# Order of the 512-column and 256-column matmuls within each piece of up-projection weights

## The chip, the cores and the metric

The kernel runs on one core of one Trainium2 chip. The metric is device time in microseconds (us), as the median of the runs made. Lower is better.

## What is computed

One transformer block on 256 rows of width 2048: three kinds of attention with gates, an output projection, and a gated feed-forward part with a causal convolution. The change lies in the feed-forward part, of which the reference says

```python
h2 = rms_norm(x, g_ffn[l])
u = causal_depthwise_conv(h2 @ w_up[l], conv_w[l], conv_b[l])
u_gate, u_val = jnp.split(u, 2, axis=-1)
x = x + (jax.nn.silu(u_gate) * u_val) @ w_down[l]
```

`h2` is 256 x 2048, `w_up` 2048 x 11264, `w_down` 5632 x 2048, all in fp32.

## The kernel before

**Split operands.** Every operand of a big product is split into two parts of the reduced-precision type `float32r`: `hi` is the rounded value and `lo` the rest. A product is then hi x hi + hi x lo + lo x hi. Weights arrive in pieces of 128 x 1024 numbers (512 KB): `piece` issues the DMA into `raw` on SP's queue (L135), casts it to `hi` on ScalarE (L136) and subtracts to get `lo` on VectorE (L137). There are four buffers of each of `raw`, `hi` and `lo`.

**The up projection** (the stage called u, tiles `u`, `hi_u`, `lo_u`, `raw_u`; L729 to L745). It works transposed: the weights are the stationary operand, the hidden rows `hT` the moving one. For each of the 16 blocks of the depth 2048, `hT[:, k, :]` has 512 columns, the 256 hi ones and then the 256 lo ones. So one matmul with `hi` weights over 512 columns (L739) makes hi x hi in the first half of a PSUM bank and hi x lo in the second half; one matmul with `lo` weights over the 256 hi columns (L740) adds lo x hi to the first half. The two halves are added later.

The loops, from outside: 11 steps `f0` of four column blocks; `s` = 0 for the gate half and 1 for the value half (22 groups in all); eight pieces per group, each holding two depth blocks `j` of 512 weight columns; in a piece, four column blocks `i`, each with a PSUM bank of its own. A piece is thus 16 matmuls, eight of 512 columns and eight of 256, each with its own load of 128 x 128 weights: 176 pieces, 1408 + 1408 matmuls.

**After a group**, `conv` (L706 to L727) takes each of the four banks: ScalarE copies the second half (L710), VectorE adds the first (L712) and multiplies by the row norms (L713), three instructions apply the taps (L716 on ScalarE, L717 and L718 on VectorE), then silu (L720) or the product with the gate half (L724) and a split into `aT` (L169, L170). These steps are queued by `later` and handed out by `tick`, which runs once per piece.

**What sets the order.** TensorE, ScalarE and VectorE each run their own queue in order. The program is written in one order, and the framework's scheduler may move instructions of different tiles past each other on an engine, by times that it works out itself. So an edit of TensorE's order can shift what stands in ScalarE's and VectorE's queues. A cast into a `hi` or `lo` buffer waits until TensorE has read the buffer's earlier contents. There are eight PSUM banks; a group takes four, so a bank is needed again two groups later.

After the u stage comes the down projection (tiles `x`, `y`, `hi_d`, `lo_d`; L796 to L844), with 512-column matmuls throughout. Ahead of it lie the attention stages; the gate products (tiles `g`, L147 to L149) are 512-column matmuls in a row, and the last projection of the second attention (tile `s`, L147 to L149) has a part that is 256 columns wide, 96 such matmuls in a row.

Of the kernel before, what the change touches and what calls it, by code (L numbers as in the profile page):

```python
# [16 lines left out]
S = 256  # L17
NT = S // P
D = 2048
KT = D // P  # L20
# [21 lines left out]
def hybrid_block(  # L42
# [25 lines left out]
    nc = tc.nc  # L68
# [12 lines left out]
    def bank(name):  # L81
        return pp.tile([P, 512], F32, tag="bank", name=name)
# [14 lines left out]
    def later(gen):  # L97
        waiting.append(gen)

    def tick():  # L100
        while waiting and len(active) < WINDOW:
            active.append([waiting.popleft(), 0])
        for a in list(active):
            if a[1] > 0:
                a[1] -= 1
                continue
            try:
                a[1] = next(a[0]) or 0
            except StopIteration:
                active.remove(a)  # L110
# [19 lines left out]
    def piece(src, a, n, name):  # L130
        raw = wp.tile([P, PIECE], F32, tag="raw", name=f"raw_{name}")
        hi = wp.tile([P, PIECE], F32R, tag="hi", bufs=SBUFS, name=f"hi_{name}")
        lo = wp.tile([P, PIECE], F32R, tag="lo", bufs=SBUFS, name=f"lo_{name}")
        m = a * n
        nc.sync.dma_start(raw[:, :m].rearrange("p (a n) -> p a n", a=a), src)  # L135
        pin(nc.scalar.copy(hi[:, :m], raw[:, :m]))  # L136
        pin(nc.vector.tensor_tensor(lo[:, :m], raw[:, :m], hi[:, :m].bitcast(F32), ALU.subtract))  # L137
        return (
            hi[:, :m].rearrange("p (a n) -> p a n", a=a),
            lo[:, :m].rearrange("p (a n) -> p a n", a=a),  # L140
        )
# [9 lines left out]
    def product(x_of, w, nk, n0, n, name):  # L151

        ps = [bank(f"{name}_{t}") for t in range(NT)]
        wv = w.rearrange("(k p) n -> p k n", p=P)
        for k in range(0, nk, 2):
            a = min(2, nk - k)
            wh, wl = piece(wv[:, k : k + a, n0 : n0 + n], a, n, f"{name}_{k}")
            order = [(j, t) for j in range(a) for t in range(NT)]
            if k + a == nk:
                order.sort(key=lambda jt: jt[1])  # L160
            for j, t in order:
                passes(ps[t][:, :n], x_of(k + j), t, wh[:, j], wl[:, j], k + j == 0, k + j == nk - 1)
            tick()
        return ps
# [278 lines left out]
    ps = proj(C_MQ, MEM_W, "mq")  # L443
# [33 lines left out]
    for c in range(3):  # L477
        ps = proj(c * 512, 512, f"f{c}")
# [7 lines left out]
    ps = proj(1536, 512, "f3")  # L486
# [3 lines left out]
    ps = proj(2048, 262, "f4")  # L490
# [68 lines left out]
    for c in range(3):  # L559
        ps = proj(C_SB + c * 512, 512, f"s{c}")  # L560
# [4 lines left out]
    ps = proj(C_SB + 1536, 512, "s3")  # L565
# [3 lines left out]
    ps = proj(C_SB + 2048, 256, "s4")  # L569
# [61 lines left out]
    for n in range(4):  # L631
        n0 = n * 512
        gate = []
        for b in range(3):
            bg = gp.tile([P, 512], F32, tag="bg", name=f"bg_{n}_{b}")
            nc.sync.dma_start(bg, b_gate[0, b, n0 : n0 + 512].partition_broadcast(P))
            ps = proj(C_GATE + b * D + n0, 512, f"g{n}_{b}")
# [11 lines left out]
        for i, (w, k0, nk, b) in enumerate(branches):  # L649
            ps = product(lambda k: oT[:, k0 + k], w[0], nk, n0, 512, f"b{n}_{b}")  # L650
# [10 lines left out]
    hT = xt_pool.tile([P, KT, 2 * S], F32R, tag="xt", name="hT")  # L661
# [19 lines left out]
    for n in range(4):  # L681
        c = slice(n * 512, (n + 1) * 512)
        ps = product(lambda k: mT[k // 2][:, k % 2], w_out[0], KT, n * 512, 512, f"o{n}")
# [21 lines left out]
    def conv(ps, f, s):  # L705
        if not pads:  # L706
            padded()
        ct = s * FT + f
        cr = cp.tile([P, S], F32, tag="cr", bufs=2, name=f"cr_{f}_{s}")
        nc.scalar.copy(cr, ps[:, S:])  # L710
        u = pads[f % 2]
        nc.vector.tensor_tensor(cr, cr, ps[:, :S], ALU.add)  # L712
        nc.vector.tensor_tensor(u[:, 2:], cr, rbc, ALU.mult)  # L713
        y = cp.tile([P, S], F32, tag="y", bufs=6, name=f"y_{f}_{s}")
        tap = lambda j: taps[:, j, ct : ct + 1]
        nc.scalar.activation(y, u[:, 2:], AF.Identity, scale=tap(2), bias=tap(3))  # L716
        nc.vector.scalar_tensor_tensor(y, u[:, 1 : S + 1], tap(1), y, ALU.mult, ALU.add)  # L717
        nc.vector.scalar_tensor_tensor(y, u[:, 0:S], tap(0), y, ALU.mult, ALU.add)  # L718
        if s == 0:
            nc.scalar.activation(y, y, AF.Silu)  # L720
            ys[f] = y
        else:
            g = ys.pop(f)
            nc.vector.tensor_tensor(g, g, y, ALU.mult)  # L724
            split_to(aT[:, f, :], g)
        return
        yield  # L727

    for f0 in range(0, FT, 4):  # L729
        for s in range(2):  # L730
            ps = [bank(f"u{f0 + i}_{s}") for i in range(4)]
            c0 = s * D_FF + f0 * P
            for k in range(0, KT, 2):
                hi, lo = piece(upv[:, k : k + 2, c0 : c0 + 512], 2, 512, f"u{f0}_{s}_{k}")
                for j in range(2):
                    first, last = k + j == 0, k + j == KT - 1
                    for i in range(4):
                        c = slice(i * P, (i + 1) * P)
                        nc.tensor.matmul(ps[i], lhsT=hi[:, j, c], rhs=hT[:, k + j, :], start=first, stop=False)  # L739
                        nc.tensor.matmul(  # L740
                            ps[i][:, :S], lhsT=lo[:, j, c], rhs=hT[:, k + j, :S], start=False, stop=last
                        )
                tick()
            for i in range(4):
                later(conv(ps[i], f0 + i, s))  # L745
# [180 lines left out]
```

## Time and profile before

| | |
|---|---|
| median of 3 runs | 1499.82 us (1497.26 to 1500.45) |
| span of the profiled execution, first to last instruction | 1494.4 us |
| TensorE clock granted over the span | 1.000 |
| TensorE weight loads busy | 84% |
| VectorE busy, ScalarE busy | 68%, 53% |
| HBM read | 280.23 MB, 189 GB/s over the span |

The profile is of one execution. What the whole execution takes beyond the span is not on the page; against the median of the runs it is 1499.82 - 1494.4 = 5.4 us. In the profile a matmul's duration is a latency: the next one starts long before the last has ended, so the pace of a stream of matmuls is the distance from one start to the next, not the duration. PE stands for matmuls, PEld for weight loads, DVE for VectorE, ACT for ScalarE.

### The profile page before, as it was taken

Reading aid. Unit: us, or ns where it says so; the run is one execution under the profiler, and the core shown is the slowest. Engines: PE = TensorE matmul, PEld = TensorE weight load, DVE = VectorE, ACT = ScalarE, POOL = GpSimd, SP = SyncE. Lnnn points to the kernel's source line nnn. Section 1 sums busy time; section 2 is a strip of 40 time slices with the busy share of each in tenths; the row PEclk is TensorE's granted clock in tenths of the full one; section 3 lists DMA queues with packets and bytes.
Section 4 is the critical chain, followed back from the end, with each engine's and each line's share of the span. In section 5 each row is a group of like instructions: output and inputs, shape, how many; then the busy total and the mean of one; then the engine's idle time right before and its main releaser. Section 6 shows DMA issues by size and latency. Waiting matters only on the chain.

```text
span 1494.4 us, 19871 instructions
## 1 busy us (share of the span) xinstructions
PE 1483.2 (99%) x7429; PEld 1255.9 (84%) x7429; DVE 1014.0 (68%) x1465; ACT 794.0 (53%) x1108; POOL 16.1 (1%) x46
## 2 busy tenths in 40 slices
PE   8999999999999999999999999999999999999998
PEld 6888888888888888888888888888888888888777
DVE  5767566555655646555557778777778778987885
ACT  6755454358544444444456556556556656553552
POOL 0000000001000000000000000000000000000000
PEclk9999999999999999999999999999999999999999
DMA  8665475365666666655555665655656565556554
GB/s 291 193 211 158 126 220 167 119 211 164 188 194 210 185 210 203 185 190 190 184 182 183 198 191 184 196 190 184 198 187 191 186 196 183 199 188 228 185 202 140
DMA packets 138543, 283.62 MB, mean 190 GB/s; under 512 B 9275, under 2 KB 18127, under 8 KB 138447
## 3 DMA queue, kind: packets, MB, share of 16 engines
q1 hardware_dynamic: 137118, 280.26, 59.0%
q10 hardware_dynamic: 1328, 2.11, 0.4%
q8 instruction: 58, 0.95, 0.2%
q14 instruction: 39, 0.31, 0.1%
HBM read 280.23 MB, written 2.10 MB: 189 GB/s over the span
## 4 chain that ended last, share of the span: by engine, by line
PE 95%; DMA 2%; ACT 1%; DVE 1%; issue 0%; POOL 0%; SPq 0%; DVEq 0%; POOLq 0%; ACTq 0%
PE u L739 21%; PE u L740 11%; PE g L147 5%; PE g L148 5%; PE g L149 5%; PE x L797 4%; PE x L798 4%; PE x L799 4%; PE s L147 2%; PE s L149 2%; PE f L147 2%; PE f L149 2%; PE s L148 2%; PE f L148 2%; PE o L147 2%; PE o L149 2%
## 5 line engine op out<-in xcount | busy, mean ns | idle before, releaser
L739 PE MATMUL u<-hT,hi_u 128*128 128x512 f32 x1408 | 488.5, 392 | 0.0
L740 PE MATMUL u<-hT,lo_u 128*128 128x256 f32 x1408 | 395.1, 281 | 0.0
L739 PEld LDWEIGHTS u<-hT,hi_u 128*128 128x128 f32 x1408 | 263.3, 187 | 57.3
L137 DVE TENSOR_TENSOR lo_u<-raw_u,hi_u 128x1024 fp32r<-128x1024 f32 x176 | 215.4, 1224 | 116.0 <-ACT hi_u L136 115.9
L740 PEld LDWEIGHTS u<-hT,lo_u 128*128 128x128 f32 x1408 | 266.8, 189 | 0.0
L136 ACT CAST hi_u<-raw_u 128x1024 fp32r<-128x1024 f32 x176 | 184.7, 1050 | 138.4 <-PE u L739 106.5
L137 DVE TENSOR_TENSOR lo_g<-raw_g,hi_g 128x1024 fp32r<-128x1024 f32 x96 | 117.7, 1229 | 101.3 <-ACT hi_g L136 98.8
L136 ACT CAST hi_g<-raw_g 128x1024 fp32r<-128x1024 f32 x96 | 100.7, 1051 | 121.8 <-PE g L148 97.4
L147 PE MATMUL g<-hi_g,xT 128*128 128x512 f32 x384 | 151.1, 393 | 0.0
L149 PE MATMUL g<-lo_g,xT 128*128 128x512 f32 x384 | 149.8, 390 | 0.0
L148 PE MATMUL g<-hi_g,xT 128*128 128x512 f32 x384 | 149.7, 390 | 0.0
L792 ACT CAST hi_d<-raw_d 128x1024 fp32r<-128x1024 f32 (+1 forms) x88 | 86.7, 993 | 74.6 <-PE x L798 38.7
L793 DVE TENSOR_TENSOR lo_d<-raw_d,hi_d 128x1024 fp32r<-128x1024 f32 (+1 forms) x88 | 99.8, 1148 | 16.2 <-ACT hi_d L792 16.2
L797 PE MATMUL x<-hi_d,aT 128*128 128x512 f32 x268 | 104.4, 390 | 0.0
L799 PE MATMUL x<-lo_d,aT 128*128 128x512 f32 x268 | 104.4, 390 | 0.0
L798 PE MATMUL x<-hi_d,aT 128*128 128x512 f32 x268 | 104.4, 390 | 0.0
L149 PEld LDWEIGHTS g<-lo_g,xT 128*128 128x128 f32 x384 | 72.1, 188 | 15.2
L148 PEld LDWEIGHTS g<-hi_g,xT 128*128 128x128 f32 x384 | 72.2, 188 | 14.5
L147 PEld LDWEIGHTS g<-hi_g,xT 128*128 128x128 f32 x384 | 72.2, 188 | 14.6
L137 DVE TENSOR_TENSOR lo_s<-raw_s,hi_s 128x1024 fp32r<-128x1024 f32 (+1 forms) x40 | 44.7, 1118 | 37.2 <-ACT hi_s L136 37.2
L137 DVE TENSOR_TENSOR lo_f<-raw_f,hi_f 128x1024 fp32r<-128x1024 f32 (+1 forms) x40 | 44.7, 1120 | 34.5 <-ACT hi_f L136 33.0
L136 ACT CAST hi_f<-raw_f 128x1024 fp32r<-128x1024 f32 (+1 forms) x40 | 38.5, 966 | 52.5 <-PE f L148 47.6
(318 smaller groups left out, 2554.3 us busy)
## 6 DMA issues: line engine op xcount, KB each, us to landing
raw_u<-in_w_up_dram SPq DMA_DIRECT2D x176, 512.0 KB, 4.0
raw_g<-in_w_in_dram SPq DMA_DIRECT2D x96, 512.0 KB, 3.6
raw_d<-in_w_down_dram SPq DMA_DIRECT2D x88, 512.0 KB, 4.7
raw_f<-in_w_in_dram SPq DMA_DIRECT2D x32, 512.0 KB, 3.5
raw_s<-in_w_in_dram SPq DMA_DIRECT2D x32, 512.0 KB, 3.4
raw_o<-in_w_out_dram SPq DMA_DIRECT2D x32, 512.0 KB, 4.7
raw_kv<-in_w_mem_kv_dram SPq DMA_DIRECT2D x15, 512.0 KB, 5.4
raw_b<-in_w_br_fox_dram SPq DMA_DIRECT2D x12, 512.0 KB, 4.0
```

Of the source, the lines that this page charges most:

```text
L136: pin(nc.scalar.copy(hi[:, :m], raw[:, :m]))
L137: pin(nc.vector.tensor_tensor(lo[:, :m], raw[:, :m], hi[:, :m].bitcast(F32), ALU.subtract))
L147: nc.tensor.matmul(o, lhsT=xh, rhs=wh, start=first, stop=False)
L148: nc.tensor.matmul(o, lhsT=xl, rhs=wh, start=False, stop=False)
L149: nc.tensor.matmul(o, lhsT=xh, rhs=wl, start=False, stop=last)
L739: nc.tensor.matmul(ps[i], lhsT=hi[:, j, c], rhs=hT[:, k + j, :], start=first, stop=False)
L740: nc.tensor.matmul(ps[i][:, :S], lhsT=lo[:, j, c], rhs=hT[:, k + j, :S], start=False, stop=last)
L792: nc.scalar.copy(hi[:, :n], src)
L793: nc.vector.tensor_tensor(lo[:, :n], src, hi[:, :n].bitcast(F32), ALU.subtract)
L797: nc.tensor.matmul(o, lhsT=ah, rhs=w[0], start=first, stop=False)
L798: nc.tensor.matmul(o, lhsT=al, rhs=w[0], start=False, stop=False)
L799: nc.tensor.matmul(o, lhsT=ah, rhs=w[1], start=False, stop=last)
```

## The change

Within each piece of up-projection weights all eight 512-column matmuls (`hi` weights) are issued first and then the eight 256-column ones (`lo` weights). Only in the last piece of a group does the order go by depth block: four of 512, four of 256, and the same again. Before, the two kinds alternated. The number of matmuls, of loads, of DMAs and of every other instruction stays as it was. The changed lines L741 and L743 are the old L739 and L740; later lines move down by three.

```diff
-                for j in range(2):
+                end = k + 2 == KT
+                for j, part in [(0, 0), (0, 1), (1, 0), (1, 1)] if end else [(0, 0), (1, 0), (0, 1), (1, 1)]:
                     first, last = k + j == 0, k + j == KT - 1
                     for i in range(4):
                         c = slice(i * P, (i + 1) * P)
-                        nc.tensor.matmul(ps[i], lhsT=hi[:, j, c], rhs=hT[:, k + j, :], start=first, stop=False)
-                        nc.tensor.matmul(
-                            ps[i][:, :S], lhsT=lo[:, j, c], rhs=hT[:, k + j, :S], start=False, stop=last
-                        )
+                        if part == 0:
+                            nc.tensor.matmul(ps[i], lhsT=hi[:, j, c], rhs=hT[:, k + j, :], start=first, stop=False)
+                        else:
+                            nc.tensor.matmul(
+                                ps[i][:, :S], lhsT=lo[:, j, c], rhs=hT[:, k + j, :S], start=False, stop=last
+                            )
```

On TensorE, half of a middle piece of the group whose tiles are `u_1_9075` to `u_1_9078` (the four banks; `hi_u_1_12`, `lo_u_1_12` are the piece) before:

```order
L739 MATMUL u_1_9075<-hT,hi_u_1_12_9248 128x512
L740 MATMUL u_1_9075<-hT,lo_u_1_12_9249 128x256
L739 MATMUL u_1_9076<-hT,hi_u_1_12_9248 128x512
L740 MATMUL u_1_9076<-hT,lo_u_1_12_9249 128x256
L739 MATMUL u_1_9077<-hT,hi_u_1_12_9248 128x512
L740 MATMUL u_1_9077<-hT,lo_u_1_12_9249 128x256
L739 MATMUL u_1_9078<-hT,hi_u_1_12_9248 128x512
L740 MATMUL u_1_9078<-hT,lo_u_1_12_9249 128x256
```

and in the change, the second half of the 512-column run and the first half of the 256-column run of the same piece:

```order
L741 MATMUL u_1_9075<-hT,hi_u_1_12_9248 128x512
L741 MATMUL u_1_9076<-hT,hi_u_1_12_9248 128x512
L741 MATMUL u_1_9077<-hT,hi_u_1_12_9248 128x512
L741 MATMUL u_1_9078<-hT,hi_u_1_12_9248 128x512
L743 MATMUL u_1_9075<-hT,lo_u_1_12_9249 128x256
L743 MATMUL u_1_9076<-hT,lo_u_1_12_9249 128x256
L743 MATMUL u_1_9077<-hT,lo_u_1_12_9249 128x256
L743 MATMUL u_1_9078<-hT,lo_u_1_12_9249 128x256
```

The first use of `lo` moved from the second place of a piece to the ninth, the last use of `hi` from the fifteenth place to the eighth, and a matmul no longer follows one that wrote the same bank.

On VectorE, where a gate group (banks `u_0_9291`, `u_0_9292`) has ended and its convolution begins among the casts of the next group's pieces (`lo_u_1_4` to `lo_u_1_8`), the scheduler's order changes as follows:

```order
 L137 TENSOR_TENSOR lo_u_1_4_9601<-raw_u_1_4_9599,hi_u_1_4_9600 128x1024
+L137 TENSOR_TENSOR lo_u_1_6_9623<-raw_u_1_6_9621,hi_u_1_6_9622 128x1024
 L712 TENSOR_TENSOR cr_0_9541<-cr_0_9541,u_0_9291 128x256
 L712 TENSOR_TENSOR cr_0_9550<-cr_0_9550,u_0_9292 128x256
 L713 TENSOR_TENSOR u_6457<-cr_0_9541,rbc 128x256
 L713 TENSOR_TENSOR u_6459<-cr_0_9550,rbc 128x256
-L137 TENSOR_TENSOR lo_u_1_6_9623<-raw_u_1_6_9621,hi_u_1_6_9622 128x1024
+L137 TENSOR_TENSOR lo_u_1_8_9645<-raw_u_1_8_9643,hi_u_1_8_9644 128x1024
```

One cast has moved ahead of the group's convolution steps, and ScalarE's casts (L136) have moved by one place in the same way. SP's order of loads is unchanged. Beyond the u stage, TensorE's order differs in a single place, where a few `lo` matmuls of the down projection's `y` and `x` tiles stand some places later; VectorE's and ScalarE's orders agree again soon after the stage's end.

## The prediction

> **What bounds the kernel now.** I read the page first, then the list of TensorE's waits, then the up-projection stage by itself. The page has TensorE at 99% and the granted clock in the top step in every slice.
>
> ```profile
> PE 1483.2 (99%) x7429; PEld 1255.9 (84%) x7429; DVE 1014.0 (68%) x1465; ACT 794.0 (53%) x1108; POOL 16.1 (1%) x46
> PEclk9999999999999999999999999999999999999999
> ```
>
> The list of what TensorE's matmuls waited for, over the whole span, names who waited, for whom, and us in total, times, longest:
>
> ```profile
> PE y L799 <- DVE lo_t L793: 2.2, 2, 1.4
> PE spare L91 <- DVE qscale L233: 1.2, 1, 1.2
> PE mT L184 <- DMA memres<-in_mem_dram: 1.2, 1, 1.2
> PE kv L147 <- ACT hi_kv L136: 1.0, 1, 1.0
> PE kv L149 <- DVE lo_kv L137: 0.5, 1, 0.5
> PE kv L147 <- ACT memT L172: 0.2, 1, 0.2
> ```
>
> All six, 6.3 us together, lie at the kernel's start (`spare`, `mT`, `kv`) or in the down projection (`y`). None is in the u stage. The stretch view of that stage (stretch, length, then busy time of PE, PEld, DVE, ACT, POOL, granted clock, DMA share, GB/s) says the same: 489.30 us, and a matmul in flight for all of it.
>
> ```profile
> 766.00:1255.30 489.30, 489.30 (x2827) 431.87 (x2826) 366.57 (x607) 289.76 (x443) 0.00 (x0) 1.00 0.60 189
> ```
>
> So there is no wait that a new order could take away. VectorE (366.57 us) and ScalarE (289.76 us) have room, and they wait for TensorE rather than the other way round: in the stage, casts into `hi` wait for the matmuls that still read the buffer.
>
> ```profile
> ACT hi_u L136 <- PE u L739: 99.6, 89, 1.7
> DVE lo_u L137 <- ACT hi_u L136: 104.1, 102, 1.8
> ```
>
> What is left to ask is whether the same 2816 matmuls run at another pace in the new order. A busy PE does not tell that, since a matmul's duration (0.39 or 0.28 us) is a latency; the distance between starts does.
>
> **The change, part by part: the pace.** In the alternating order the stretch from 800 to 1250 us gives the pace without rounding. This row is of the 512-column line, with count, durations, and first and last start; below it, from the timeline, stand its first and last instance, and three neighbours elsewhere.
>
> ```profile
> L739 PE MATMUL u<-hT,hi_u x1299: 390/391/392, 799.8 to 1249.8; 128*128 128x512 f32 x186
> 799.81 0.39 PE L739 MATMUL u<-hT,hi_u 128*128 128x512 f32 x1
> 1249.78 0.39 PE L739 MATMUL u<-hT,hi_u 128*128 128x512 f32 x1
> ...
> 900.00 0.39 PE L739 MATMUL u<-hT,hi_u 128*128 128x512 f32 x1
> 900.23 0.28 PE L740 MATMUL u<-hT,lo_u 128*128 128x256 f32 x1
> 900.34 0.39 PE L739 MATMUL u<-hT,hi_u 128*128 128x512 f32 x1
> ```
>
> A pair takes (1249.78 - 799.81) / 1298 = 346.7 ns. The neighbours split it: 230 ns from a 512-column start to the 256-column one, hence 116.7 ns back.
>
> The new order makes steps from 512 to 512 and from 256 to 256, and the trace of before holds long runs of both, each matmul with a weight load of its own as here. The gate products are 512 columns in a row. These are the third line of their triples, and its first and last instance:
>
> ```profile
> L149 PE MATMUL g<-lo_g,xT x76: 387/390/391, 426.2 to 477.2; 128*128 128x512 f32 x76
> 426.18 0.39 PE L149 MATMUL g<-lo_g,xT 128*128 128x512 f32 x1
> 477.22 0.39 PE L149 MATMUL g<-lo_g,xT 128*128 128x512 f32 x1
> ```
>
> 75 triples are 225 steps: 51.04 / 225 = 226.8 ns a step. The narrow part of projection `s` is 256 columns in a row, again in triples; its third line, with the weight loads of that line, and the first and last instance:
>
> ```profile
> L149 PEld LDWEIGHTS s<-lo_s,xT x28: 191/192/193, 299.8 to 309.5; 128*128 128x128 f32 x28
> L149 PE MATMUL s<-lo_s,xT x28: 282/284/284, 299.9 to 309.6; 128*128 128x256 f32 x28
> 299.88 0.28 PE L149 MATMUL s<-lo_s,xT 128*128 128x256 f32 x1
> 309.61 0.28 PE L149 MATMUL s<-lo_s,xT 128*128 128x256 f32 x1
> ```
>
> 27 triples are 81 steps: 9.73 / 81 = 120.1 ns a step. The two like-to-like steps together make 226.8 + 120.1 = 346.9 ns, against 346.7 ns for the two mixed ones: +0.2 ns.
>
> How many are exchanged? A middle piece had eight steps of each mixed kind, counting the step into the next piece. Now it has seven from 512 to 512, one to 256, seven from 256 to 256, and one back: seven pairs exchanged. A group's last piece has two runs of four, so six. With 22 groups of seven middle pieces and one last, that is 154 x 7 + 22 x 6 = 1210 exchanged pairs. The sum is 1210 x 0.2 ns = **+0.24 us**, or nothing.
>
> No run shows the two kinds of step mixed in the new proportion, so I bound each exchanged pair by the steps seen: at least 226.8 + 116.7 = 343.5 ns (-3.2 ns, -3.9 us in all), at most 230 + 120.1 = 350.1 ns (+3.4 ns, +4.1 us). I take the middle, because whole runs of 225 and 81 steps carry the sum and single starts the ends.
>
> **The casts.** Moving the first use of `lo` from the second place of a piece to the ninth gives VectorE about 7 x 227 = 1.6 us more time, and releasing `hi` seven places early lets ScalarE's cast into that buffer start about 0.8 us sooner (seven steps of 120 ns). Neither is worth anything, because the casts already lie far ahead. The tightest place that recurs is the fifth piece after a value group; there the `lo` cast and the piece's first `lo` matmul are
>
> ```profile
> 906.58 1.22 DVE L137 TENSOR_TENSOR lo_u<-raw_u,hi_u 128x1024 fp32r<-128x1024 f32 x1
> 911.67 0.28 PE L740 MATMUL u<-hT,lo_u 128*128 128x256 f32 x1
> ```
>
> so the cast ends at 907.80, 3.9 us early. It would cost something only with that cover gone. The loads on SP's queue wait for VectorE to free `raw`; their order is the same, their release the same or earlier, so they cost nothing.
>
> **The convolution steps** are what comes later. One cast now stands ahead of them in both queues. That `lo` cast waits until the group's last matmul has read its buffer, then runs 1.22 us; before, ScalarE's first copy and VectorE's first add ran in the group's last microsecond:
>
> ```profile
> 899.50 0.72 ACT L710 COPY cr<-u 128x256 f32<-128x256 f32 x2 [0.80 <-PE u L740]
> 899.91 0.77 DVE L712 TENSOR_TENSOR cr<-cr,u 128x256 f32<-128x256 f32 x2
> 906.25 0.42 DVE L712 TENSOR_TENSOR cr<-cr,u 128x256 f32<-128x256 f32 x1
> ```
>
> The group ends at 900.34, so the last bank is read out 6.3 us into the next group; I estimate 2 us of delay from the moved cast and the first bank's later end (0.7 us at most: three 512-column steps now lie between its last two matmuls). The banks are needed again when the next group has ended, 8 x 8 x 346.7 ns = 22.2 us after this one. About 14 us remain: cost zero. At the stage's end the list shows no wait of the first down-projection matmuls, so I put zero there too. The place beyond it where a few `lo` matmuls move back has no wait of before that I could tie to it.
>
> **Rivals.** *Slower: the weight loads starve in runs of short matmuls.* A load starts when the matmul ahead of it starts, and lasts 187 to 193 ns by the rows:
>
> ```profile
> 900.23 0.19 PEld L739 LDWEIGHTS u<-hT,hi_u 128*128 128x128 f32 x1
> ```
>
> If a load had to end before the next matmul, a run of 256-column steps would go at 190 ns instead of 120, and 1210 x 70 ns = 85 us would be lost, for about 1584 us. It decides as soon as the part of a load that cannot overlap exceeds the 120 ns step. Against it: that row's load starts at 900.23 and its matmul at 900.34, and projection `s` sustains 120.1 ns with loads of 192 ns. A mild form, a few ns per step, is the upper bound above: 1504 us. The Trainium skill, page "TensorE: Matmul & The Clock Gate", section "LDWEIGHTS (loading the stationary operand)", puts a load at its columns divided by 1.2, an estimate of 107 ns for 128 columns, which would leave next to nothing under a 256-column matmul and speaks for caution with eight in a row. By that figure a run of short steps would still fit 120 ns and the sum would stay +0.24 us; the trace's `s` rows agree that it fits, while its rows of 187 to 193 ns show latency rather than that price.
>
> *Faster: a matmul that follows one into the same bank pays for it.* The step from 512 to 256, into the same bank, is 230 ns where 512 to 512 takes 226.8. If that is a price of the bank, it goes, and the pairs run at 343.5 ns: -3.9 us, 1495.9 us. Against it: the triples of `g` and `s` also write one bank three times in a row, at 226.8 and 120.1 ns, and what the first step loses the second (116.7) gives back.
>
> *Slower: the convolution runs late* and a bank or `aT` is missed. It needs 14 us of delay where I see 2; with 16 us it would cost some 2 us at each of 20 groups, 40 us, 1540 us.
>
> *The change doesn't act at all*, because the scheduler restores the order, is excluded: TensorE's rows stand in the new order.
>
> **How the numbers follow.** The profiled execution's span becomes 1494.4 + 0.24 = 1494.6 us; with the 5.4 us to the median the forecast is 1499.82 + 0.24 = **1500.1 us**. Chances: forecast, within 3 us of before, 0.84; starved loads, mild or strong, 0.07; late convolution 0.02; bank price 0.07. The range takes in the bounds of the step: 1499.8 - 3.9 = 1495.9 to 1499.8 + 4.1 = 1503.9; the strong forms lie outside and hold under 0.1. A measurement of this kernel can tell about 0.2%, 3 us, from no change. So faster 0.07, within 0.2% 0.84, slower 0.09.
>
> **What would show it.** In the profile after: like-to-like steps near 227 and 120 ns, the u stage at 489 to 490 us, and no wait of TensorE in it. A 256-column step above 123 ns shows the starved loads, below 118 the bank price; a wait of `u` for ScalarE or VectorE shows the late convolution. I am wrong if the short runs pace differently in u, where the two depth blocks' `hT` columns are re-read, than in `s`.

## The result, and the profile after

The changed kernel is slower: 1504.26 us (median of 7 runs, 1502.08 to 1505.24) against 1498.64 us (7 runs, 1497.26 to 1500.63), a ratio of 1.0032, with a 95% interval of 1.0021 to 1.0043, or 3.1 to 6.4 us. The forecast was 1500.1 us.

The page after still shows one engine at its limit.

```profile
PE 1488.8 (99%) x7429; PEld 1258.0 (84%) x7429; DVE 1009.1 (67%) x1465; ACT 792.0 (53%) x1108; POOL 16.2 (1%) x46
```

The profiled execution took 1505.24 us with a span of 1503.6 us. That is 9.2 us more than the span before, which overstates the change: the medians lie 5.6 us apart. Each profiled execution from here on took 1.6 to 1.9 us more as a whole than its span; by that, an estimate, the first profile of before is of an execution of some 1496 us, 2.5 us quicker than the median of seven. So most of the 5.4 us between span and median was that one execution's luck, and not time beyond its span. A second profile of the unchanged kernel was therefore taken among the experiments (span 1498.1 us). This table splits the three spans by the first and the last start of a matmul of the u stage:

| us | before | before, again | after |
|---|---|---|---|
| start of the span to the first u matmul | 766.0 | 764.5 | 764.4 |
| first to last start of the u stage | 489.19 | 489.19 | 492.87 |
| last u start to the last matmul's start | 234.4 | 239.6 | 241.4 |

Only the middle row is the same to 0.01 us in both executions of the old kernel, and only there is the loss clean: **+3.68 us**. The tile rows of u in the trace after (count, least, median and greatest duration in ns, first and last start in us) give its ends:

```profile
L741 PE MATMUL u<-hT,hi_u x1408: 386/393/478, 764.4 to 1256.7; 128*128 128x512 f32 x176
L743 PE MATMUL u<-hT,lo_u x1408: 277/283/284, 766.2 to 1257.3; 128*128 128x256 f32 x176
```

The stretch view of the stage (columns as in the prediction) shows that no new wait made it:

```profile
764.40:1257.40 493.00, 493.00 (x2827) 433.59 (x2826) 361.87 (x605) 287.22 (x442) 0.00 (x0) 1.00 0.65 188
```

A matmul is in flight for all of the 493.00 us and the granted clock is 1.00, as before. The page's groups have no idle time ahead of either line (the last column), though their busy time now says little, since overlapping matmuls of one line merge:

```profile
L741 PE MATMUL u<-hT,hi_u 128*128 128x512 f32 x1408 | 356.8, 393 | 0.0
L743 PE MATMUL u<-hT,lo_u 128*128 128x256 f32 x1408 | 199.9, 282 | 0.0
```

So the pace itself is slower. In TensorE's timeline after, a row holds a whole run of one kind (start, length, count at the end of the row):

```profile
1000.27 2.00 PE L741 MATMUL u<-hT,hi_u 128*128 128x512 f32 x8
1002.11 1.12 PE L743 MATMUL u<-hT,lo_u 128*128 128x256 f32 x8
1003.06 0.63 PE L741 MATMUL u<-hT,hi_u 128*128 128x512 f32 x2
```

Eight steps from the first 512-column start to the first 256-column start take 1.84 us, 230 ns each, and the eight back take 0.95 us, 119 ns each. A piece is 2.79 us, against 8 x 346.7 ns = 2.77 us before. Finer, from the starts of all middle pieces, the mean step from each of the 16 matmuls to the next (ns):

```
after, 512 columns:  233.9  235.9  228.3  232.3  231.0  226.7  226.7  226.1
after, 256 columns:  113.9  119.1  120.1  119.8  120.2  120.1  120.0  119.4     sum 2793.3
before, all pieces:  230.0 and 116.7 in turn                                    sum 2773.3
```

From the sixth place on a 512-column run goes at the 226.7 ns that the prediction took from tile `g`, and a 256-column run at the 120.0 ns taken from tile `s`. But the first five long steps after a short run are slow: 7.2 + 9.2 + 1.6 + 5.6 + 4.3 = 28 ns above 226.7. About 7 ns come back at the start of the short run. That leaves **20 ns a piece**; a group's last piece, with two returns from short to long, loses 33 ns. 154 x 20 + 22 x 33 ns = 3.8 us, of which the first group saves 0.14 us: it took 23392 ns before and 23425 ns after, 33 ns more in place of 173, because before, too, its first matmuls ran slowly (shown behind the experiments). Every group but the first and the last takes 22360 ns from its first start to the next group's (before: 22187 ns), the same to 1 ns.

**Behind the stage** TensorE's waits from 1257 us on are

```profile
PE y L802 <- DVE lo_t L796: 6.4, 5, 2.1
PE y L800 <- ACT hi_t L795: 0.2, 1, 0.2
```

The second is new. 25 us into the down projection it comes from the u stage's last convolution steps, which are now later. The last step of all, on VectorE, in the trace before and then in the trace after:

```profile
1270.25 0.42 DVE L170 TENSOR_TENSOR aT<-y,aT 128x256 fp32r<-128x256 f32 x1
```

```profile
1273.78 0.42 DVE L170 TENSOR_TENSOR aT<-y,aT 128x256 fp32r<-128x256 f32 x1 [0.47 <-ACT aT L169]
```

Counted from the first down-projection matmul (1255.33 before, 1257.41 after), it ends at 15.34 us before and at 16.79 us after, 1.45 us later. The steps and casts that follow on VectorE and ScalarE (tiles `fw`, `fr`, `t`, `hi_t`) shift with it. Before, the second cast into `hi_t` ended at 1279.34, 1.2 us ahead of the matmul that needs it:

```profile
1278.28 1.06 ACT L792 CAST hi_t<-t 128x1024 fp32r<-128x1024 f32 x1 [2.84 <-DVE t L833]
1280.53 0.39 PE L797 MATMUL y<-hi_t,sf 128*128 128x512 f32 x1
```

After, it ends 1.44 us later against the first down-projection matmul, which is too late for TensorE:

```profile
1281.81 1.06 ACT L795 CAST hi_t<-t 128x1024 fp32r<-128x1024 f32 x1 [2.01 <-DVE t L836]
```

```profile
1282.37 0.39 PE L802 MATMUL y<-lo_t,sf 128*128 128x512 f32 x1
1282.92 0.50 PE L800 MATMUL y<-hi_t,sf 128*128 128x512 f32 x1 [0.16 <-ACT hi_t L795]
1283.26 0.39 PE L801 MATMUL y<-hi_t,sf 128*128 128x512 f32 x1
1283.49 0.40 PE L800 MATMUL x<-hi_t,aT 128*128 128x512 f32 x1
1283.72 0.39 PE L801 MATMUL x<-hi_t,aT 128*128 128x512 f32 x1
1283.95 0.42 PE L800 MATMUL x<-hi_d,aT 128*128 128x512 f32 x1
1284.21 0.48 PE L802 MATMUL y<-lo_t,sf 128*128 128x512 f32 x1
```

The steps into the waiting matmul and out of it are 550 and 340 ns where 227 is the rule, and the `lo_t` matmul of `y` stands behind four others: this is the place of the moved `lo` rows. Summed above 227 ns a step, the first 30 us of the down projection lose 0.60 us after and 0.00 before.

**The rest of the down projection** loses 9.4 us above 227 ns a step after, 3.0 us before, but 8.2 us in the second profile of before. Nearly all of it comes with waits of `y` for `lo_t` and the steps behind them; 1.6 us of the 9.4 are steps at half the clock, shown at the end. The two executions of the old kernel differ by 5.2 us in it, so no term of the change is read from it. That the change makes these waits longer as well is neither shown nor excluded. Without it the account is 3.7 + 0.6 = 4.3 us, inside the measured 3.1 to 6.4 us. Whether the other 1.3 us of the medians' 5.6 us belong to the change is not settled by these runs.

### The profile page after: what moved, and what is told of

The parts are those of the page before. It is cut to its first block, busy times and chain, and to the rows that moved or that the text cites. A ratio compares the mean times of both kernels' runs of the same rounds, so it can differ in the third digit from the quotient of the medians.

```text
span 1503.6 us, 19872 instructions
## 1 busy us (share of the span) xinstructions
PE 1488.8 (99%) x7429; PEld 1258.0 (84%) x7429; DVE 1009.1 (67%) x1465; ACT 792.0 (53%) x1108; POOL 16.2 (1%) x46
## 4 chain that ended last, share of the span: by engine, by line
PE 94%; DVE 2%; DMA 1%; ACT 1%; issue 1%; POOL 0%; SPq 0%; DVEq 0%; POOLq 0%; ACTq 0%
PE u L741 22%; PE u L743 11%; PE g L147 5%; PE g L149 5%; PE g L148 5%; PE x L801 4%; PE x L800 4%; PE x L802 4%; PE s L147 2%; PE s L149 2%; PE f L147 2%; PE f L148 2%; PE s L148 2%; PE f L149 2%; PE o L148 2%; PE o L149 2%
## 5 line engine op out<-in xcount | busy, mean ns | idle before, releaser
L741 PE MATMUL u<-hT,hi_u 128*128 128x512 f32 x1408 | 356.8, 393 | 0.0
L741 PEld LDWEIGHTS u<-hT,hi_u 128*128 128x128 f32 x1408 | 251.7, 189 | 43.7
L136 ACT CAST hi_u<-raw_u 128x1024 fp32r<-128x1024 f32 x176 | 184.4, 1048 | 185.2 <-PE u L741 123.4
L743 PEld LDWEIGHTS u<-hT,lo_u 128*128 128x128 f32 x1408 | 195.1, 190 | 15.8
L743 PE MATMUL u<-hT,lo_u 128*128 128x256 f32 x1408 | 199.9, 282 | 0.0
L137 DVE TENSOR_TENSOR lo_g<-raw_g,hi_g 128x1024 fp32r<-128x1024 f32 x96 | 117.5, 1227 | 101.5 <-ACT hi_g L136 99.1
L136 ACT CAST hi_g<-raw_g 128x1024 fp32r<-128x1024 f32 x96 | 100.8, 1052 | 121.8 <-PE g L148 96.6
L136 ACT CAST hi_f<-raw_f 128x1024 fp32r<-128x1024 f32 (+1 forms) x40 | 38.6, 967 | 52.5 <-PE f L148 47.6
```

The costliest lines, as they stand in the source:

```text
L743: nc.tensor.matmul(ps[i][:, :S], lhsT=lo[:, j, c], rhs=hT[:, k + j, :S], start=False, stop=last)
```

## The experiments

Two things were to be explained: 20 ns a piece, and 0.6 us behind the stage. The theories for the first, as the expectations name them: **A**, each exchanged pair costs some 3 ns, by a price of like-to-like steps; **B**, each return from short to long matmuls costs a fixed 17 to 20 ns; **C**, a matmul that leaves its predecessor's PSUM bank costs something. Later ones are named where they come up. Most kernels replace the changed kernel's two inner loops over the 16 matmuls of a piece with one loop over a list of (depth block `j`, column block `i`, `part`: 0 for `hi`, 1 for `lo`), and the diffs are cut to the line with that list, or to the first lines that set the order. Each of these kernels ran once, so the stage and the group decide, and the whole times, each beside one execution of the old kernel on the same chip, only go with them. "Group" is the time from one group's first start to the next, in the regular groups: 22187 ns before, 22360 ns after.

### Runs of four

```diff
+                for j, i, part in [(j, i, p) for j in range(2) for p in range(2) for i in range(4)]:
```

> Every piece goes by depth block: four of 512, four of 256, four of 512, four of 256 (the changed kernel's last piece of a group, now for all). From first to last matmul start the up-projection stage took 489.2 us before and 492.9 us in the changed kernel. Theory A, each exchanged pair of like-to-like steps costs the same 3.1 ns: 6 pairs a piece x 176 x 3.1 ns = 3.3 us, stage 492.5 us. Theory B, each return from a run of 256-column matmuls to a run of 512-column ones costs 16 to 20 ns, whatever the runs' length from four on: two returns a piece, 352 x 16 ns = 5.6 us, stage 494.8 us. Theory C, it is the bank: what keeps the alternating order cheap is that the 256-column matmul follows into the bank just written: 15 of 16 steps leave the bank as in the changed kernel, stage 492.9 us.

Its u tiles:

```profile
L739 PE MATMUL u<-hT,hi_u x1408: 387/396/486, 764.9 to 1259.2; 128*128 128x512 f32 x176
L741 PE MATMUL u<-hT,lo_u x1408: 277/281/285, 765.8 to 1259.8; 128*128 128x256 f32 x176
```

The stage takes 494.89 us, the group 22453 ns, 33.3 ns a piece more than before; the whole 1504.85 us, beside 1500.10 us for the kernel before on the same chip. More returns cost more although fewer pairs are exchanged, as B has it, and against A.

### Runs of sixteen

```diff
-            for k in range(0, KT, 2):
-                hi, lo = piece(upv[:, k : k + 2, c0 : c0 + 512], 2, 512, f"u{f0}_{s}_{k}")
+            for k0 in range(0, KT, 4):
+                two = [piece(upv[:, k : k + 2, c0 : c0 + 512], 2, 512, f"u{f0}_{s}_{k}") for k in (k0, k0 + 2)]
+                for part in range(2):
+                    for q in range(4):
+                        k, w = k0 + q, two[q // 2][part]
```

> Two pieces are taken together: sixteen of 512, then sixteen of 256. Theory A (3.1 ns per exchanged pair): 15 pairs per two pieces, 88 x 15 x 3.1 ns = 4.1 us, stage 493.3 us. Theory B (16 to 20 ns per return to a run of 512): half a return a piece, 88 x 20 ns = 1.8 us, stage 491.0 us. Theory C (leaving the bank): as the changed kernel or a little more, 492.9 us and up. The down projection's order is that of before here; if the few moved rows there cost the changed kernel anything, this run does without it.

The stage takes 490.82 us, the group 22267 ns: 80 ns more than before for four returns, 20 ns each. The long run's steps are 233.4, 235.8, 228.3, 232.5, 230.8 and then eleven of 226.7 ns. So the loss is in the first five steps and does not grow with the run: B again. The whole took 1502.14 us beside 1500.10.

### Runs of two

```diff
+                for j, i, part in [(j, i + d, p) for j in range(2) for i in (0, 2) for p in range(2) for d in range(2)]:
```

> Runs of two: two of 512, two of 256, and so on. Theory A: four exchanged pairs a piece, 176 x 4 x 3.1 ns = 2.2 us, stage 491.4 us. Theory B: four returns a piece; if a return costs 16 ns for runs of two as well, 11 us, stage 500 us; if the price only builds up over a run, less, down to nothing. Theory C: every step but none stays in its bank, as the changed kernel, 492.9 us.

The stage takes 491.44 us, the group 22293 ns; whole 1500.35 us beside 1500.10. This is the number of A, and far below four times B's price a piece. Its steps, from the starts, are 232.5, 230.8, 113.3, 119.2, 233.3, 235.8, 115.8, 112.4 ns, and round again: 3.3 ns for each cycle of two long and two short. With the two runs above, A cannot be meant; what falls is that B's price is one constant. It is 20 ns where the runs are long enough, 16.7 ns for runs of four and 3.3 ns for runs of two.

### Alternation, `lo` one block behind

Within a piece the `lo` matmul of a block follows the `hi` matmul of the next one. Long and short alternate, but no matmul follows one of its own bank; one long step stands double at the piece's start and one short at its end.

```diff
+                for j, i, part in [(0, 0, 0)] + [x for n in range(7) for x in (((n + 1) // 4, (n + 1) % 4, 0), (n // 4, n % 4, 1))] + [(1, 3, 1)]:
```

> Alternating as before, but the 256-column matmul runs one column block behind, so that no matmul follows into the bank just written except at the end of a piece, while no two of a kind are neighbours except there (one pair a piece). Theory A: one exchanged pair a piece, 176 x 3.1 ns = 0.5 us, stage 489.7 us. Theory B: next to nothing, runs of one, 489.2 to 489.7 us. Theory C: the saving of the same bank is gone, 492.9 us or more.

The stage takes 497.24 us, the group 22560 ns, and the whole 1507.10 us beside 1500.10, more than A and B gave and the dearest order of this set. It spoke for C at the time; the last experiments show why it doesn't.

### The same order with zeros

Is it an electrical effect, by which the array is slower on dense data (theory **P**), or the sequence alone (**S**)?

```diff
-    gffn = lambda k: gmix_c[:, KT + k : KT + k + 1]
+    none = cst.tile([P, 1], F32, name="none")
+    nc.vector.memset(none, 0.0)
+    gffn = lambda k: none
```

> The changed kernel with the hidden rows multiplied by zero ahead of the up projection (the feed-forward part is so left without its input): the same instructions on all-zero moving data. The runs so far bear out theory B (a fixed loss of some 20 ns at each return from 256 to 512 columns). Theory P, the loss is electrical, the clock giving way as the array's load steps up: with zeros it is gone, stage 489.2 us. Theory S, it is a matter of sequence and addresses: the steps are the same to the ns, stage 492.9 us.

A piece in its timeline:

```profile
1000.33 2.00 PE L743 MATMUL u<-hT,hi_u 128*128 128x512 f32 x8
1002.17 1.11 PE L745 MATMUL u<-hT,lo_u 128*128 128x256 f32 x8
1003.12 0.63 PE L743 MATMUL u<-hT,hi_u 128*128 128x512 f32 x2
```

The same 1.84 and 0.95 us with every moving number zero; the stage 492.88 us, the group 22360 ns, the whole 1504.92 us beside 1496.99. P falls.

### The same order with one length

```diff
-                                ps[i][:, :S], lhsT=lo[:, j, c], rhs=hT[:, k + j, :S], start=False, stop=last
+                                ps[i], lhsT=lo[:, j, c], rhs=hT[:, k + j, :], start=False, stop=last
```

> The changed kernel's order, but the matmuls with the lo weights run over all 512 columns too (a fourth product, lo x lo, is added). No change of length is left, all else of the order stays. If the change of length makes the loss, every step is 226.7 ns, stage 2816 x 226.7 = 638.4 us. If leaving the bank at every step makes it, steps stay above that at least at the start of each run; at 3 ns a step 646 us.

The 16 matmuls of a piece, in the timeline:

```profile
1000.44 1.98 PE L743 MATMUL u<-hT,lo_u 128*128 128x512 f32 x8
1002.25 1.52 PE L741 MATMUL u<-hT,hi_u 128*128 128x512 f32 x6
```

Eight steps take 1.81 us, and from the starts every one of the 16 takes 226.7 ns; the stage is 639.25 us (whole 1649.32 us), 0.85 us above the forecast, as the first group also holds the eight transposes that it has in every kernel. The changed order of banks and weights, with one length throughout, costs nothing. So the loss needs two lengths.

### Alternation into one bank, across depth blocks

Is it that the long and the short step of a pair no longer stream the same block of `hT` (theory **E**)? Here they stream different blocks, yet the bank and the lengths go as before.

```diff
+                for j, i, part in [x for j in range(2) for i in range(4) for x in ((j, i, 0), (1 - j, i, 1))] if k + 2 < KT else [(j, i, p) for j in range(2) for i in range(4) for p in range(2)]:
```

> Alternating, each 256-column matmul into the bank that the 512-column one has just written, but from the other depth block: the bank is kept as before, and the block of hidden rows that streams changes at each step (last piece of a group as before). The shifted order of the earlier run kept the streaming block and left the bank, and cost 8.0 us. Theory C (leaving the bank after one matmul, with lengths mixed, costs): stage 489.2 us. Theory E (order of streaming blocks or of weight addresses costs): some 8 us more, 497 us.

```profile
L739 PE MATMUL u<-hT,hi_u x1408: 389/391/476, 764.8 to 1253.7; 128*128 128x512 f32 x176
L741 PE MATMUL u<-hT,lo_u x1408: 277/280/284, 765.0 to 1254.0; 128*128 128x256 f32 x176
```

The stage takes 489.19 us and the group 22187 ns, both as before; whole 1495.26 us beside 1496.99. E falls.

### Runs of eight, each bank twice in a row

```diff
+                for j, i, part in [(j, i, p) for p in range(2) for i in range(4) for j in range(2)]:
```

> Eight of 512 and then eight of 256 as in the changed kernel, but both depth blocks of a column block follow each other, so that every bank is written twice in a row and the streaming block changes at each step. Theory C: half as many departures from a bank; the transient at the start of a run should shrink, stage 491 us or less, 489.2 if writing a bank twice is enough. Theory B alone (the change of length, whatever the banks): 154 x 20 + 22 x 20 ns = 3.5 us, stage 492.7 us.

The stage takes 492.57 us, the group 22347 ns: eight returns at 20 ns. The steps are those of the changed kernel (233.3, 235.8, 228.3, 232.5, 230.8, 226.7 ns and on), though every second one stays in its bank. B holds without any part of C. The whole took 1503.62 us beside 1496.99.

### The kernel before, unchanged

> The kernel before, unchanged, profiled a second time. The up-projection stage should again take 489.2 us. From the last up-projection matmul to the last of the kernel its first profile took 234.4 us, the changed kernel's 241.5 us. If that difference belongs to the change, this run shows about 234.5 again. If it is a matter of how fast the weights of the second half of the down projection land in a given execution, it may be 236 to 240 us, with TensorE's waits for the lo cast of the sums (longest group of waits in that stage) at 4 us and more.

The stage again takes 489.19 us and the group 22187 ns. The waits behind it do not repeat: where the first profile had 2.2 us in 2 waits, this one has

```profile
PE y L799 <- DVE lo_t L793: 6.7, 6, 2.2
```

with a whole time of 1499.92 us beside 1498.47. This is what takes the down projection's second half out of the account above.

### The changed order, the last group alternating

Does the late convolution of the last group make the 0.6 us behind the stage?

```diff
+                if f0 + 4 >= FT and s == 1:
+                    order = [(j, i, p) for j in range(2) for i in range(4) for p in range(2)]
```

> The changed kernel, but the very last group of the up projection alternates as before. Up-projection stage: one group less at its loss of 173 ns, 492.7 us. Theory: the 0.6 us that the changed kernel lost some 25 us into the down projection come from the last group's convolution running 1.5 to 2 us late on VectorE; then they are gone here, no step there above its 227 ns by more than 25 ns in the first half of the down projection. Rival: they come from the earlier groups' order (the casts' place in the queues); then 0.3 to 0.7 us stay.

Yes: the wait of `y` for `hi_t` is gone, TensorE's order in the down projection is that of before, and the first 30 us lose 0.02 us instead of 0.60. The whole took 1502.73 us beside 1498.47. Across all kernels the 0.6 us (0.58 to 0.60) stand in exactly the four that have the moved `lo` rows and this wait: the change, the runs of four, the zeros and the one length. Lateness is enough for such a loss, without moved rows: in the kernel with each bank twice in a row TensorE's order there is that of before, the cast into `hi_t` ends 0.5 us later than before, and 0.32 us are lost at the same place. How much of the 0.6 us the moved rows add is not separated.

The stage held a surprise. It takes 493.12 us, not the 492.7 that one alternating group should have brought. In that group, three pairs:

```profile
1240.20 0.40 PE L745 MATMUL u<-hT,hi_u 128*128 128x512 f32 x1
...
1241.26 0.40 PE L745 MATMUL u<-hT,hi_u 128*128 128x512 f32 x1
```

That is 1.06 us for three pairs, 353 ns each, where the same alternation takes 346.7 ns before. The group's 127 steps take 22493 ns, against 22070 ns for the last group before.

### Strict alternation through the group, `lo` one block behind

C against a theory **L**: alternation has a second, slower pace, into which a doubled length puts it. Here only a group's first long and last short step are double; in between, long and short alternate for 16 depth blocks.

```diff
+                        nc.tensor.matmul(ps[i], lhsT=hi[:, j, c], rhs=hT[:, k + j, :], start=k + j == 0, stop=False)
+                        if behind:
+                            small(*behind.pop())
+                        behind.append((lo, k, j, i))
```

> Strictly alternating within a whole group, the 256-column matmul always one column block behind, across pieces too: every step leaves the bank, and the only neighbours of a kind are the first two and the last two of a group. The shifted order of the fourth run had such a pair in every piece and cost 8.0 us. Theory L (only the sequence of lengths counts): one disturbance per group instead of eight; if it dies out within some steps, 22 x 20 to 46 ns, stage 489.6 to 490.2 us; if it lasts as long as the alternation goes on, up to 497 us. Theory C (leaving the bank): 497 us. Against C stands already that banks written twice in a row changed no step by more than 1 ns.

Three pairs in the middle of a group:

```profile
1000.22 0.40 PE L745 MATMUL u<-hT,hi_u 128*128 128x512 f32 x1
1000.45 0.28 PE L736 MATMUL u<-hT,lo_u 128*128 128x256 f32 x1
1000.57 0.40 PE L745 MATMUL u<-hT,hi_u 128*128 128x512 f32 x1
1000.80 0.28 PE L736 MATMUL u<-hT,lo_u 128*128 128x256 f32 x1
1000.91 0.40 PE L745 MATMUL u<-hT,hi_u 128*128 128x512 f32 x1
1001.16 0.28 PE L736 MATMUL u<-hT,lo_u 128*128 128x256 f32 x1
1001.28 0.40 PE L745 MATMUL u<-hT,hi_u 128*128 128x512 f32 x1
```

Again 1.06 us. The steps go round in threes of pairs, 232.5 + 117.5, 240.8 + 120.0, 235.8 + 113.4 ns, 1060 ns instead of 1040, from the group's third step to its end. The group takes 22613 ns, which is 22187 + 64 x 6.67; the stage 498.44 us; the whole 1507.55 us beside 1498.47. Alone this run leaves C open, since its matmuls all leave their bank.

### The order of before with one dent

Every `lo` matmul follows its own bank's `hi` matmul, except that in each piece one pair of long and one of short matmuls stand double.

```diff
+                for j, i, part in [(0, 0, 0), (0, 0, 1), (0, 1, 0), (0, 1, 1), (0, 2, 0), (0, 3, 0), (0, 2, 1), (0, 3, 1)] + [(1, i, p) for i in range(4) for p in range(2)]:
```

> Alternating into the same bank as before, with one doubled pair in the middle of each piece (two of 512, then two of 256). Theory L (lengths alone): a disturbance per piece as in the shifted order; between the 13 ns a piece of the runs of two (stage 491.5 us) and the 46 ns of the shifted order (497.2 us), by how long the alternation takes to come back to 230 and 116.7 ns. Theory C (bank): only 3 of 16 steps leave the same-bank pattern, at 5.7 ns a pair about 1 to 2 us, stage 490 to 491 us.

Three pairs that alternate in one bank each, some steps behind a dent:

```profile
1000.05 0.40 PE L739 MATMUL u<-hT,hi_u 128*128 128x512 f32 x1
...
1001.12 0.40 PE L739 MATMUL u<-hT,hi_u 128*128 128x512 f32 x1
```

1.07 us. The same values of a step appear as in the run before (232.5, 117.5, 240.8, 120.0, 235.8, 113.3 ns), though these pairs keep their bank; from dent to dent the pieces differ, and some pairs after a dent go at 231 + 113 ns, for the moment faster than before. The group takes 22373 ns, 186 more than before, the stage 493.18 us, the whole 1505.58 us beside 1498.47. With the runs of eight in one bank, which cost as much as those that leave it, C falls; L holds.

**The trace of before had it already.** It enters the u stage straight from a run of 512-column matmuls of tile `o`. Its first pairs, before the eight transposes of 128 columns that write `hT` at 771.66 us:

```profile
770.25 0.40 PE L739 MATMUL u<-hT,hi_u 128*128 128x512 f32 x1
...
771.31 0.40 PE L739 MATMUL u<-hT,hi_u 128*128 128x512 f32 x1
```

1.06 us for three pairs, in the unchanged order and each pair in its own bank. Behind the transposes the pace is 346.7 ns a pair and stays so to the end of the stage. In the kernel with `lo` behind within a piece, the steps after the same transposes are 230 and 117 ns until its next doubled length, and at the slow pace after it: 7 pairs x 6.67 ns x 176 pieces = 8.2 us, against 8.05 us measured. In the two last kernels the transposes do not restore the faster pace. What sets which pace follows them is open.

The orders together:

| order of lengths in a piece | stage, us | group, ns | above before, a piece |
|---|---|---|---|
| before; across depth blocks | 489.19 | 22187 | 0 |
| runs of 16 | 490.82 | 22267 | 10.0 |
| runs of 2 | 491.44 | 22293 | 13.3 |
| runs of 8, each bank twice in a row | 492.57 | 22347 | 20.0 |
| the change; with zeros | 492.87; 492.88 | 22360 | 21.6 |
| one dent | 493.18 | 22373 | 23.3 |
| runs of 4 | 494.89 | 22453 | 33.3 |
| `lo` one block behind, in a piece | 497.24 | 22560 | 46.6 |
| `lo` one block behind, in a group | 498.44 | 22613 | 53.3 |

No order tried goes faster than the strict alternation of before.

## Why the prediction was wrong

The forecast was no change within 0.2%, with 0.84; measured are +0.32% (0.21 to 0.43). The median after, 1504.26 us, lies 0.4 us beyond the range's end. As a change that end, +4.1 us, lies inside the measured 3.1 to 6.4 us. That the number came so close is luck: that end comes from putting the old mixed step's 230 ns for every long step, and not from the settling that made the loss.

**Bound and waits: right.** There was no wait in the stage to take away and none came; TensorE is in flight for 493.00 of 493.00 us.

**The pace: the step that failed.** It put each exchanged pair at 226.8 + 120.1 = 346.9 ns, +0.24 us in all, taking the paces of runs without end of tiles `g` and `s` for runs of eight. Both paces are right where a run has settled. But a run of eight spends five of its eight long steps settling. The mean step from 512 to 512 in the stage after is 231.0 ns and from 256 to 256 it is 119.0 ns, 350.0 ns a pair: +3.3 ns in place of +0.2, 1210 x 3.3 ns = 4.0 us, where the whole stage measured +3.68 us (492.87 us, against the 489 to 490 that were to show the forecast). The rest is in the first group and in the mixed steps left, which became shorter: 226.1 + 119.4 ns in a middle piece. This is the text's upper bound, 350.1 ns, reached by another way than its wording. I chose the middle "because whole runs of 225 and 81 steps carry the sum"; just their length made them unlike the new order.

**What should have warned.** The settling itself stands in the trace of before, right behind the run of `s` from which the pace of 120.1 ns was taken. The last 256-column matmul of `s` is followed by `g`:

```profile
309.61 0.28 PE L149 MATMUL s<-lo_s,xT 128*128 128x256 f32 x1
309.73 0.40 PE L147 MATMUL g<-hi_g,xT 128*128 128x512 f32 x1
...
310.89 0.39 PE L149 MATMUL g<-lo_g,xT 128*128 128x512 f32 x1
```

Five steps from 309.73 to 310.89 are 1.16 us, 232 ns each. From the starts they are 234, 235, 229, 232 and 231 ns, and then 226 and 227: the slow steps of the new order to 1 ns, some 27 ns above 226.7 in all. That is the price before the 7 ns that the next short run gives back. The prediction counted one step back per piece, but priced it like the old mixed step and the long steps behind it like settled ones.

The mixed step was measured from 800 to 1250 us alone. The same line runs at 353 ns a pair between 766 and 771 us. Two paces for one sequence of instructions in one trace say that a step depends on more than its own kind and its neighbour's, so that no sum of steps taken from elsewhere is safe to 3 ns.

**The casts: right.** They cost nothing; no matmul of u waits for one.

**The convolution: right in the stage, wrong at its end.** The estimate of 2 us of delay fits the 1.45 us measured at the end, and the cover of 14 us held within the stage. But "zero" at the stage's end rested on the first down-projection matmuls, and the wait came 25 us later, through the steps that follow the convolution: 0.6 us, tied to it by the run that lets the last group alternate. The moved `lo` rows, to which the prediction could tie no wait, stand right there.

**Rivals.** *Starved loads*: the 256-column step settles at 120.0 ns and its mean is 119.0, below the 123 ns set as the sign; the slow steps are the long ones. The strong form is excluded, and the mild form's 1504 us was met by another cause. The Trainium skill, page "TensorE: Matmul & The Clock Gate", section "LDWEIGHTS (loading the stationary operand)", by whose columns over 1.2 I estimated 107 ns, would let a load fit such a step; the trace agrees that it fits. *Bank price*: excluded by the kernel with each bank twice in a row. Its sign, a 256-column step below 118 ns, did appear, in the first step of each short run (113.9 ns), but it stands in that kernel too (113.3 ns). *Late convolution*: the mechanism exists, at 0.6 us instead of 40, and at the end only. *The change doesn't act*: excluded as said.

**The sum.** 0.24 us forecast; +3.7 us of pace and +0.6 us of late convolution shown; +5.6 us between the medians, with 3.1 to 6.4 us as the interval. The range ended at 1503.9 us because it held the pace's upper bound and nothing beside it. The second, small loss was the one it had no room for.

**Open.** What in TensorE makes the settling and the two paces, and the 1.3 us between the account and the medians. The first lies in the sequence of lengths, and neither in the data, nor the bank, nor the block that is streamed.

## What to carry to other kernels

A pace taken from a long uniform run holds for a short run only after its first steps; where an order mixes lengths, compare whole periods, and look in the trace for a second place where the same sequence runs at another pace, or where lengths change as they will in the new order. Grouping like matmuls is no gain in itself: here strict alternation of 512 and 256 columns was the fastest of the orders tried. A delay at a stage's end should be followed through the steps behind it to the first matmul that needs them, and not only to the next matmul.

## What the runs showed of the hardware

- A step's length depends on what ran before it, at least five matmuls back. After a run of short matmuls, 512-column steps take 233.3, 235.8, 228.3, 232.5 and 230.8 ns before they settle at 226.7 ns, with all moving data zero as well.
- A strict alternation of 512 and 256 columns held two paces here, 346.7 and 353.3 ns a pair. The slower goes round in three pairs. It lasted 63 pairs without a change, and in the trace before it ended at eight 128-column matmuls, which did not bring the faster pace in the two last kernels.
- Behind a wait of 2.1 us in the down projection after, steps of 427 ns appear in place of 227, eight in all:

```profile
1396.93 0.51 PE L802 MATMUL y<-lo_t,sf 128*128 128x512 f32 x1 [2.10 <-DVE lo_t L796]
...
1398.35 0.63 PE L800 MATMUL x<-hi_d,aT 128*128 128x512 f32 x1
1398.78 0.63 PE L801 MATMUL x<-hi_d,aT 128*128 128x512 f32 x1
1399.21 0.63 PE L802 MATMUL x<-lo_d,aT 128*128 128x512 f32 x1
```

  The granted clock of the stretch from 1396 to 1400 us is 0.69:

```profile
1396.00:1400.00 4.00, 3.07 (x8) 2.47 (x9) 4.00 (x5) 1.05 (x1) 0.00 (x0) 0.69 0.24 46
```

  The steps cost 8 x 0.2 = 1.6 us. Six to twelve such steps stand in five other kernels, none in either profile of before, and hardly any behind waits as long in others, so this case does not show what brings them. The six kernels with them show a mean clock of 0.998 or 0.999 over the span, those without show 1.000. Three further executions of the old kernel, beside the experiments, have 0.999, which speaks against the change as their cause. Nor do they explain the medians: of the seven runs of the change the three at 1.000 took 1502.08 to 1504.71 us and the four below it 1503.35 to 1505.24.
